# A staging transfer in two parts: four channels at the head of ScalarE's queue, four at its tail

## The chip, the cores and the metric

The kernel runs on one core of a Trainium2 chip. The time is the device time of one launch in microseconds (us). The core has engines that copy data in its on-chip memory (DVE, called VectorE, and ACT, called ScalarE), a third one (POOL, GpSimd) that here only issues transfers, and SP, which only issues transfers too. Transfers between the chip's main memory (DRAM) and the on-chip memory are carried by 16 DMA engines that all issuers share. Each issuer has a queue of its own; in the profile q10 is ScalarE's, q1 is SP's and q0 is POOL's.

## The reference

`x` holds 16 images of 64 channels of 64 x 64 float32 values. The result holds, for each of 15 x 15 window positions, the 8 x 8 window of all 64 channels; neighbouring windows overlap by half.

```python
n_h = (h - window_size) // stride + 1      # 15
n_w = (w - window_size) // stride + 1      # 15
for i in range(n_h):
    for j in range(n_w):
        result[:, i, j] = x[:, :, i*4 : i*4 + 8, j*4 : j*4 + 8]
```

There is no arithmetic. 16.8 MB are read and 59.0 MB are written (16 x 15 x 15 x 64 x 64 values of 4 bytes); the work is to cut windows out of rows and to lay them one after the other.

## The kernel before

The on-chip memory has 128 partitions. The tile `Lt` (viewed as `L`) holds all of `x`: partition = half of the channels (`ch`, 2) x group of eight images (`y`, 2) x image in the group (8) x quarter of the rows (`q`, 4), and in each partition 32 channels of 16 rows of 64 values. So one channel of one image and one quarter is a run of 4 KB in DRAM and in `L`.

Loading has two ways.

- Most channels are loaded straight into `L` by the function `load` (line 61). SP's queue takes channels 10 to 31 of the first half (`ch` 0), POOL's queue takes channels 8 and 9 of the first half and channels 7 to 31 of the second. These run over `y` and, inside, over `q`: first all four quarters of the first eight images, then those of the last eight. SP issues 14 of them and POOL 16.
- The first eight channels of the first half and the first seven of the second (`FC = (8, 7)`) are *staged*: they are loaded into the tile `GG` by eight transfers (line 129), one per quarter and half, each over all 16 images. The four transfers of `ch` 0 (8 channels, 512 KB each) are issued by ScalarE, the four of `ch` 1 (7 channels, 448 KB each) by SP. They stand at the head of both queues. Staged channels are then *moved* from `GG` into `L` by 16 copies of at most two channels (`moves`, line 148): first the four of `y` 0, `ch` 0, then `y` 0, `ch` 1, then the same for `y` 1. Every third of these copies, beginning with the first, is done by ACT, the others by DVE. A copy takes all four quarters of its two channels, so it waits for all four transfers of its half.

Windows are then gathered from `L` into output tiles, which lie in the same `GG` (the first three have 4096 values per partition, the later ones 6144, three at a time in rotation), and stored. The function `first` (line 200) fills the first three tiles with eight copies each, `plain` (line 245) and `cross` (lines 157, 258, 262) the following ones, `second` (line 228) two late ones; all of these are stored by POOL with an indirect transfer (`scatter`, line 165). The last two tiles (line 290) are stored by SP (line 291). `first` reads rows of the first eight images (`y` 0) of both halves, so it waits for the direct loads of `y` 0 and for their moves; and since its tiles lie where staged channels lay, it also waits for the moves that read those.

The order on each engine is that of the program text for the copies marked `keep_in_program_order`. A transfer's completion is counted in a semaphore. SP and ScalarE together have eight such semaphores, given out in the order of the program: the ninth transfer takes the first one's, and is issued only when that earlier transfer has landed. POOL has eight of its own.

The lines that matter below are 124 (the views `S` of the staged channels), 126 to 129 (the staging transfers), 61 (direct loads), 148 (moves), 200 and 165 (first tiles and their stores). `TC`, the name that the change uses, is 4: the number of channels whose run of 1024 values makes up one tile of 4096.

Of the kernel before, what the change touches and what calls it, by code (L numbers as in the profile page):

```python
# [10 lines left out]
def kernel(  # L11
# [7 lines left out]
    nc = tc.nc  # L19
    P = nc.NUM_PARTITIONS  # L20

    B, C, H, W = x.shape
# [8 lines left out]
    CH = 2  # L31
    HQ = P // (B * CH)
# [8 lines left out]
    QP = YB * HQ  # L41
# [75 lines left out]
    TC = CFREE // (RB * W)  # L117


    FC = (8, 7)  # L120
# [2 lines left out]
    assert sum(FC) * CP <= NG * LF  # L123
    S = [GG[:, ch * FC[0] * CP : (ch * FC[0] + FC[ch]) * CP].rearrange("p (c f) -> p c f", c=FC[ch])[:, :, 0 : RB * W].rearrange("p c (r w) -> p c r w", r=RB) for ch in range(CH)]
    x_b = x.rearrange("b (ch cl) (hq r) w -> ch hq b cl (r w)", ch=CH, hq=HQ)
    for q in range(HQ):
        for ch in range(CH):
            s = S[ch][QP + q : QP + q + (B - 1) * HQ + 1 : HQ]
            (nc.scalar, nc.sync)[ch].dma_start(out=s, in_=x_b[ch, q, :, 0 : FC[ch], :])

# [194 lines left out]
```

## Time and profile before

| | |
|---|---|
| time, median of 3 runs | 184.44 us (184.37 to 184.56) |
| the profiled execution's own time | 184.26 us |
| its span (first to last instruction) | 182.4 us |
| busy: DVE, ACT, POOL | 137.2, 138.5, 39.7 us |
| DMA: moved in the span, mean rate | 75.80 MB, 416 GB/s |

The profiled execution spends 1.86 us outside its span. The kernel's time in other runs lies up to 0.3 us above that execution's. "DMA share" in a table of stretches is the mean busy share of the 16 DMA engines; it can read a little above 1, since packets that follow one another overlap in the records by a few nanoseconds. A row of the timeline gives start, length, engine, line, operation, output and input, count, and in brackets the idle time before it and what ended it.

### The profile page before, as it was taken

To read this page: it belongs to the slowest core of one execution; us is meant where nothing else is said; L and a number is where in the kernel's file an instruction comes from. 1 tells how busy PE (TensorE), PEld (TensorE's weight loads), DVE (VectorE), ACT (ScalarE), POOL (GpSimd) and SP (SyncE) were. 2 spreads that over 40 slices of the span, in tenths; PEclk is the share of its full clock that TensorE was granted. 3 is DMA by queue.
4 is the path that set the end of the run, shared out by engine and by line. 5 is a ranking of instruction groups with operands and counts; after the bars stand their busy time and mean duration, and the time that the engine had idled before them with its cause. 6 is when DMAs were issued, how large, how long until landed. Compare 5 with 4: busy or idle time off the path is not lost.

```text
span 182.4 us, 445 instructions
## 1 busy us (share of the span) xinstructions
DVE 137.2 (75%) x138; ACT 138.5 (76%) x60; POOL 39.7 (22%) x41
## 2 busy tenths in 40 slices
DVE  4003997999995969769979979889597996996600
ACT  0003998999949978769969969889699999998600
POOL 7501553033220220220220221022207025140000
DMA  5999999999999999999999999999999999999995
GB/s 157 406 412 411 410 412 410 410 412 445 420 438 449 431 437 431 431 431 428 431 431 431 431 431 422 431 437 431 431 426 431 431 431 437 426 431 431 431 431 226
DMA packets 9363, 75.80 MB, mean 416 GB/s; under 512 B 2736, under 2 KB 2736, under 8 KB 6832
## 3 DMA queue, kind: packets, MB, share of 16 engines
q0 software_dynamic: 6592, 62.92, 81.4%
q1 hardware_dynamic: 2192, 10.75, 14.3%
q10 hardware_dynamic: 576, 2.10, 3.1%
q14 instruction: 3, 0.02, 0.0%
HBM read 16.78 MB, written 62.91 MB: 437 GB/s over the span
## 4 chain that ended last, share of the span: by engine, by line
DMA 72%; DVE 14%; issue 5%; POOL 2%; DVEq 1%; POOLq 0%; PEldq 0%
DMA out_dram<-GG,idx 23%; DMA out_dram<-GG,idx_lo 22%; DMA Lt<-in_x_dram 20%; DVE GG L157 7%; DMA out_dram<-GG,idx_hi 6%; DVE GG L200 2%; DVE GG L262 2%; POOL Lt L61 2%; DVE GG L290 2%; DVE GG L245 1%; DVEq L322 1%; DVE GG L228 0%; DVEq L245 0%; POOL pi L77 0%; DVEq L157 0%
## 5 line engine op out<-in xcount | busy, mean ns | idle before, releaser
L258 ACT COPY GG<-Lt 64x4096 f32<-64x4096 f32 (+1 forms) x20 | 55.0, 2750 | 9.7 <-DMA out_dram<-GG,idx_lo 6.2
L157 DVE STREAM_SHUFFLE GG<-Lt 64x2048 f32<-64x2048 f32 (+1 forms) x25 | 49.2, 1970 | 0.6
L245 ACT COPY GG<-Lt 64x4096 f32<-64x4096 f32 (+1 forms) x10 | 27.5, 2750 | 4.5 <-DMA out_dram<-GG,idx_v 2.7
L148 DVE COPY Lt<-GG 32x2048 f32<-32x2048 f32 (+1 forms) x10 | 11.3, 1180 | 13.8 <-DMA GG<-in_x_dram 13.7
L262 DVE COPY GG<-Lt 64x2048 f32<-64x2048 f32 (+1 forms) x20 | 19.1, 955 | 0.5
L200 DVE COPY GG<-Lt 32x2048 f32<-32x2048 f32 x15 | 18.3, 1219 | 1.3 <-DMA Lt<-in_x_dram 1.0
L228 ACT COPY GG<-Lt 32x4096 f32<-32x4096 f32 (+1 forms) x6 | 18.2, 3033 | 0.3 <-DMA out_dram<-GG,idx_hi 0.2
L228 DVE COPY GG<-Lt 32x2048 f32<-32x2048 f32 (+1 forms) x10 | 16.5, 1646 | 2.4 <-DMA out_dram<-GG,idx 1.4
L200 ACT COPY GG<-Lt 32x2048 f32<-32x2048 f32 x9 | 17.1, 1897 | 1.0 <-DMA Lt<-in_x_dram 0.8
L61 POOL DMA_DIRECT2D Lt<-in_x_dram x16 | 12.7, 798 | 17.1 <-DMA Lt<-in_x_dram 16.6
L165 POOL DMA_INDIRECT out_dram<-GG,idx x5 | 9.7, 1931 | 24.7 <-ACT GG L245 20.8
L148 ACT ACT_TABLE_LOAD x1 | 1.3, 1283 | 16.8 <-DMA GG<-in_x_dram 16.8
L245 DVE COPY GG<-Lt 64x4096 f32<-64x4096 f32 x5 | 11.4, 2289 | 0.2
L165 POOL DMA_INDIRECT out_dram<-GG,idx_hi x5 | 4.8, 961 | 30.5 <-DVE GG L262 30.5
L290 DVE COPY GG<-Lt 32x2560 f32<-32x2560 f32 (+1 forms) x8 | 9.2, 1152 | 1.8 <-DMA out_dram<-GG,idx 1.7
L148 ACT COPY Lt<-GG 32x2048 f32<-32x2048 f32 (+1 forms) x6 | 10.3, 1752 | 0.1
L165 POOL DMA_INDIRECT out_dram<-GG,idx_lo x5 | 4.8, 961 | 25.2 <-DVE GG L262 15.8
L290 ACT COPY GG<-Lt 32x1536 f32<-32x1536 f32 (+1 forms) x8 | 9.2, 1149 | 0.8 <-DMA out_dram<-GG,idx 0.6
L157 DVE LOAD_MASK_SELECT GG<-Lt x25 | 0.2, 9 | 12.6 <-DMA out_dram<-GG,idx_lo 7.3
L165 POOL DMA_INDIRECT out_dram<-GG,idx_v x3 | 4.5, 1512 | 14.3 <-DVE GG L200 8.7
L165 POOL DMA_INDIRECT out_dram<-GG,idx_r x2 | 2.8, 1403 | 11.7 <-ACT GG L228 11.7
L80 DVE TENSOR_SCALAR tb<-pi 128x1 int32<-128x1 int32 x1 | 0.2, 154 | 1.0 <-POOL pi L77 1.0
(24 smaller groups left out, 3.4 us busy)
## 6 DMA issues: line engine op xcount, KB each, us to landing
Lt<-in_x_dram POOLq DMA_DIRECT2D x8, 800.0 KB, 16.4
out_dram<-GG SPq DMA_DIRECT2D x2, 1536.0 KB
Lt<-in_x_dram SPq DMA_DIRECT2D x6, 384.0 KB
GG<-in_x_dram ACTq DMA_DIRECT2D x4, 512.0 KB
Lt<-in_x_dram SPq DMA_DIRECT2D x6, 320.0 KB
GG<-in_x_dram SPq DMA_DIRECT2D x4, 448.0 KB
Lt<-in_x_dram SPq DMA_DIRECT2D x2, 704.0 KB
Lt<-in_x_dram POOLq DMA_DIRECT2D x8, 64.0 KB, 16.4
```

The source lines that it names most:

```text
L61: eng.dma_start(out=L[p0 : p0 + QP - HQ + 1 : HQ, c0:c1, :, :], in_=x_v[ch, y, q, :, c0:c1, :])
L80: nc.vector.tensor_scalar(out=d[:, :], in0=pi[:, :], scalar1=shift, scalar2=mask, op0=ALU.logical_shift_right, op1=ALU.bitwise_and)
L148: tc.keep_in_program_order(copy(out=L[d, c:e, :, :], in_=S[ch][f, c:e]))
L157: return nc.vector.stream_shuffle(out=out, in_=in_, mask=mask)
L165: st = nc.gpsimd.indirect_dma_start(out=rows, out_offset=bass.IndirectOffsetOnAxis(ap=ix[:, 0:1], axis=0), in_=g, in_offset=None, element_ ...
L200: (act if n % 3 == 0 else dve)(out=g[d * QP : (d + 1) * QP, ch], in_=L[f : f + QP, :, s * ST : s * ST + WS, cols],)
L228: (act if i in (0, 5, 6) else dve)(out=g[d * QP : (d + 1) * QP, n], in_=windows(slice(f, f + QP), every, slice(s * ST, s * ST + WS), j, m),)
L245: tc.keep_in_program_order(copy(out=g[d, n], in_=windows(f, every, slice(half * ST, half * ST + WS), j, m)))
L258: act(out=g[lo, n], in_=windows(f, every, slice(s * ST, s * ST + WS), j, m))
L262: dve(out=g[hi, n, :, 0:ST], in_=windows(f, every, slice((s + 1) * ST, RB), j, m))
L290: copy(out=g[d, n, c0:c1], in_=windows(f, slice(c0, c1), slice(s * ST, s * ST + WS), j, m))
L322: with _tile.TileContext(nc) as tc:
```

## The change

ScalarE's first staging transfer (quarter 0 of `ch` 0) carries channels 0 to 3 in place of 0 to 7. Channels 4 to 7 of that quarter are carried by a fifth transfer, which ScalarE issues after its other three. SP's four staging transfers, all direct loads, the moves and everything behind them have the same text as before.

```diff
     x_b = x.rearrange("b (ch cl) (hq r) w -> ch hq b cl (r w)", ch=CH, hq=HQ)
-    for q in range(HQ):
-        for ch in range(CH):
-            s = S[ch][QP + q : QP + q + (B - 1) * HQ + 1 : HQ]
-            (nc.scalar, nc.sync)[ch].dma_start(out=s, in_=x_b[ch, q, :, 0 : FC[ch], :])
+    for q, ch, c0, c1 in [(q, ch, 0, TC if q + ch == 0 else FC[ch]) for q in range(HQ) for ch in range(CH)] + [(0, 0, TC, FC[0])]:
+        s = S[ch][QP + q : QP + q + (B - 1) * HQ + 1 : HQ, c0:c1]
+        (nc.scalar, nc.sync)[ch].dma_start(out=s, in_=x_b[ch, q, :, c0:c1, :])
```

In the built program two things follow from the count of nine transfers in place of eight ahead of the direct loads. The fifth transfer is the ninth on the eight shared semaphores, so it waits until ScalarE's first has landed; and each of SP's direct loads waits for a transfer that stands one place later in the program than before. And a copy of channels 0 to 3 now waits only for the first four transfers of ScalarE's queue, a copy of channels 4 to 7 for the last four.

## The prediction

> **What bounds the kernel now.** I read the page first, then the table of stretches, then the transfers by queue in the first microseconds, then the instructions around the staged copies. From the page, the DMA row (the span in 40 slices, busy tenths) and the rate:
>
> ```profile
> span 182.4 us, 445 instructions
> DVE 137.2 (75%) x138; ACT 138.5 (76%) x60; POOL 39.7 (22%) x41
> DMA  5999999999999999999999999999999999999995
> DMA packets 9363, 75.80 MB, mean 416 GB/s; under 512 B 2736, under 2 KB 2736, under 8 KB 6832
> DMA 72%; DVE 14%; issue 5%; POOL 2%; DVEq 1%; POOLq 0%; PEldq 0%
> ```
>
> DVE and ACT are idle a quarter of the span; the DMA engines are busy in every slice but the first and the last, and carry 72% of the chain that ended last. The table of stretches (columns: stretch, length, busy time of DVE, ACT, POOL, clock, DMA share, GB/s) says how full they are:
>
> ```profile
> 2.00:5.00 3.00, 1.08 (x11) 0.00 (x0) 3.00 (x6) 1.00 0.91 298
> 5.00:15.00 10.00, 0.00 (x0) 0.00 (x0) 2.15 (x4) 1.00 1.03 411
> 15.00:29.00 14.00, 11.35 (x10) 11.61 (x7) 5.67 (x6) 1.00 1.03 410
> 29.00:43.00 14.00, 13.44 (x12) 13.54 (x8) 3.65 (x3) 1.00 1.03 411
> 43.00:58.00 15.00, 14.26 (x10) 12.24 (x5) 3.24 (x3) 1.00 1.02 434
> 58.00:180.00 122.00, 96.16 (x87) 101.10 (x42) 21.11 (x16) 1.00 1.01 432
> ```
>
> From 5 to 180 us the share is 1.01 or more: there is no idle DMA time that an earlier copy could fill. The time is the bytes by their rate, plus what is lost at the two ends. Loads run at 411 GB/s to about 43 us, stores at 432 after that. So an edit to the loads can act in three ways only: it makes the beginning better or worse, it delays a store so far that the engines run dry, or it adds bytes. The change adds no byte.
>
> The beginning, 2 to 5 us, moves 298 GB/s where 411 is the rate later: 3.0 x (1 - 298/411) = 0.82 us are lost there in all, part of it before the first packet. That is the most that a better beginning can give. By queue (q10 ScalarE's, q1 SP's; first the answer for 2.0 to 3.8 us, then for 3.8 to 5.0):
>
> ```profile
> DMA packets 99, 0.41 MB, mean 225 GB/s; under 512 B 0, under 2 KB 0, under 8 KB 99
> q10 hardware_dynamic: 99, 0.41, 83.8%
> ```
>
> ```profile
> DMA packets 136, 0.49 MB, mean 406 GB/s; under 512 B 17, under 2 KB 17, under 8 KB 136
> q1 hardware_dynamic: 91, 0.37, 76.8%
> q10 hardware_dynamic: 45, 0.12, 24.8%
> ```
>
> Up to 3.8 us only ScalarE's first transfer moves, though SP issued its own at the same time; then SP's follows. The first transfer is the one that the change halves, so this is the place to look at.
>
> **The change part by part.** The rows of the staging transfers and of who waited for them, and those of the copies that use them:
>
> ```profile
> L129 ACTq DMA_DIRECT2D GG<-in_x_dram x4: 613/639/680, 0.7 to 2.7; - x4
> L129 SPq DMA_DIRECT2D GG<-in_x_dram x4: 694/764/812, 0.7 to 3.1; - x4
>   ACT L148: 16.8, 1
>   DVE Lt L148: 13.7, 1
> ```
>
> ```profile
> 16.83 1.28 ACT L148 ACT_TABLE_LOAD   x1 [16.83 <-DMA GG<-in_x_dram]
> 16.86 11.42 DVE L148 COPY Lt<-GG 32x2048 f32<-32x2048 f32 x10 [13.68 <-DMA GG<-in_x_dram]
> 18.13 10.40 ACT L148 COPY Lt<-GG 32x2048 f32<-32x2048 f32 x6
> 29.30 17.26 ACT L200 COPY GG<-Lt 32x2048 f32<-32x2048 f32 x9 [0.78 <-DMA Lt<-in_x_dram]
> 29.33 16.09 DVE L200 COPY GG<-Lt 32x2048 f32<-32x2048 f32 x13 [1.04 <-DMA Lt<-in_x_dram]
> ```
>
> *A fifth issue on ScalarE's queue.* One more issue of 0.64 us (median of the four). It waits until ScalarE's first transfer has landed; SP's first direct load waits for that landing now and goes out at 4.83 us, so it landed by then:
>
> ```profile
> 4.83 0.81 SPq L61 DMA_DIRECT2D Lt<-in_x_dram  x1
> 6.26 0.68 SPq L61 DMA_DIRECT2D Lt<-in_x_dram  x1
> 10.42 0.68 SPq L61 DMA_DIRECT2D Lt<-in_x_dram  x1
> ```
>
> Half as many bytes land no later, so the fifth is out by 4.83 + 0.64 = 5.5 us at the latest. Behind it on ACT stands only the table load, which waits until 16.8 us. Cost nothing; the cover is 11 us of idle ACT, and 1.31 MB that ScalarE's queue still has to move by then (2.10 less the 0.41 + 0.12 moved by 5 us and the fifth's own 0.26).
>
> *SP's direct loads wait one place later.* The first now goes when SP's own first transfer has landed, 6.26 us at the latest by the second row, in place of 4.83; the second takes the place of the third, and so on. SP's queue holds 4 x 448 KB = 1.84 MB of staging ahead of them, and by the next answer it moves 1.81 MB from 5 to 15 us, so it still has work to about 13 us. Cost nothing; by then three loads are in it (10.42 us). POOL's order and waits are unchanged.
>
> *When the staged channels arrive.* From 5 to 15 us, and from 15 to 17, the queues move (packets, MB, share):
>
> ```profile
> q1 hardware_dynamic: 506, 1.81, 45.3%
> q10 hardware_dynamic: 418, 1.55, 38.1%
> q0 software_dynamic: 475, 0.74, 19.7%
> ```
>
> ```profile
> q10 hardware_dynamic: 14, 0.02, 3.2%
> ```
>
> ScalarE's queue runs at 0.155 MB per us, and 0.26 MB of it moves from the front to the back: 1.7 us of that queue. If its end stays where it is, the first four transfers are in at 16.83 - 1.7 = 15.1 us and the fifth at 16.8; if the queue is set back by the whole of it, they are in at 16.8 and 18.5. I take the middle, 16.0 and 17.6, since SP's queue moves ahead at the start and gives the time back later. Then ACT loads its table at 16.0 and makes its first copy at 17.3, its second needs the fifth transfer (there), so it ends at 28.5 - 0.8 = 27.7. DVE makes one copy (1.2 us) at 16.0, waits to 17.6, and goes on where it now stands at 16.86 + 1.2 = 18.1: it ends at 28.3 - 0.5 = 27.8. In the late case DVE ends at 28.3 + 0.4 = 28.7, ACT where it does now.
>
> *What is late next.* Both then wait for direct loads to 29.3 us in every one of these cases, 0.5 to 1.7 us longer than now, or DVE 0.4 shorter in the late case. The loads' bytes ahead of that point are the same, on engines that are full, so 29.3 stays. The gain of 0.5 to 0.8 us is worth nothing. Even a slip there would not show at once: POOL issues the first stores at
>
> ```profile
> 36.37 1.76 POOL L165 DMA_INDIRECT out_dram<-GG,idx_v  x1 [5.60 <-DMA Lt<-in_x_dram]
> 42.50 1.81 POOL L165 DMA_INDIRECT out_dram<-GG,idx_v  x1 [4.38 <-DVE GG L200]
> 48.67 0.97 POOL L165 DMA_INDIRECT out_dram<-GG,idx_v  x1 [4.35 <-DVE GG L200]
> ```
>
> and from 38.2 to 43.4 us all 793 packets are under 8 KB, that is loads of 4 KB (the rows of a store have 16):
>
> ```profile
> DMA packets 793, 2.14 MB, mean 411 GB/s; under 512 B 272, under 2 KB 272, under 8 KB 793
> ```
>
> So the first store, issued by 38.1, starts behind the loads at about 43.4. Each holds 2.1 MB, 4.8 us at 434 GB/s: the second is needed at 48.2 and issued by 44.3, the third at 53.0 and issued by 49.6. The tightest cushion is 3.4 us; POOL's first load was issued at 1.5 us and has no packet in the answer for 2 to 5 us, so up to about 2.8 us of it can be the way from issue to packet, which leaves 0.6 us at worst.
>
> *The beginning.* ScalarE's first transfer now covers the engines for half as long: 0.26 MB at 411 GB/s is 0.64 us less. This is the one term that the trace does not show, so I bound it. From above: SP's queue might be unable to start before 3.8 us, and nothing else is there; the engines then stand from the end of the four channels to 3.8. ScalarE's queue alone had 0.41 MB done by then, so 0.26 MB at about 3.1 to 3.3, and the loss is up to 0.6 us. From below: the low rate might come of one queue working alone, and end when the second joins 0.64 us sooner. In finer stretches,
>
> ```profile
> 2.00:2.60 0.60, 0.57 (x8) 0.00 (x0) 0.60 (x2) 1.00 0.75 116
> 2.60:3.20 0.60, 0.52 (x4) 0.00 (x0) 0.60 (x2) 1.00 0.89 259
> 3.20:3.80 0.60, 0.00 (x0) 0.00 (x0) 0.60 (x2) 1.00 0.88 300
> 3.80:4.40 0.60, 0.00 (x0) 0.00 (x0) 0.60 (x2) 1.00 1.02 403
> ```
>
> the stretch 3.2 to 3.8 would run at 403 in place of 300, a gain of 0.6 x 103/411 = 0.15 us; with all that is lost after 2.6 us it is 0.6 x (152 + 111)/411 = 0.4 us. I take -0.1 us: the engines are already 0.88 busy with the one queue, and nothing shows SP's queue as not ready, since it was issued at 0.74 us like ScalarE's.
>
> Here the Trainium skill has a rule (DMA: Bandwidth & Descriptors, section Queues, rings and completion order): a DMA engine goes round the queues, but drains a whole packet, typically 9 to 17 descriptors, from one before it turns to the next. The trace agrees in that ScalarE's 512 KB, eight rows of 4 KB for each of 16 engines, go almost whole before SP's begin at 3.8 us. By the rule SP's transfer waits for its turn, not for readiness, and the first term above is 0 rather than 0.6 us; the forecast stands without it.
>
> **Sum.** Issue 0, waits 0, copies 0, beginning -0.1 (from -0.4 to +0.6): 184.26 - 0.1 for an execution like the profiled one, and against the median of the runs, 184.44, which is 0.18 above it, 184.35 us. Its own range: 184.0 to 184.7.
>
> **The rivals.** A measurement of this kernel can tell about 0.2%, 0.37 us, from no change.
>
> 1. *The engines stand at the beginning* (slower). SP's first transfer is not ready when the four channels are through, and ScalarE's second is not either. For it: no packet of SP's before 3.8 us in the trace. Against it: SP's transfer was issued 3 us before that. Price up to 0.6, likely 0.5 us: 184.9. It decides from a gap of 0.37 us.
> 2. *The moves become late* (slower). The fifth transfer shares its last stretch with POOL's queue and lands later than 18.5 us. It decides when the first gather starts more than 0.6 us after 29.3, so when DVE's moves end after 29.9, the fifth landing at about 19.7 or later; then a store is late by the excess. With a landing at 20.5 it is 0.8 us: 185.2. Against it: full engines, and no byte more ahead of it.
> 3. *The beginning gets better than I take it* (faster): one queue alone is what holds the rate at 116 to 300 GB/s. 0.4 us less: 184.0. For it: 403 GB/s as soon as SP's queue joins. Against: the rate climbs while ScalarE's queue is still alone, so time has a part in it.
> 4. *The smaller transfer costs its fixed time on the engines* (slower). SP's first direct load goes 4.83 - 0.74 = 4.1 us after the transfer whose landing it awaits was issued, and 0.52 MB at 411 GB/s are 1.3 of them; if a transfer's remaining 2.8 us occupied engines, one more transfer would give 187.2. Against it: share 1.03 at 411 GB/s from 5 to 15 us, with transfers of three queues in flight, so this time is covered. The Trainium skill (same page, section Anatomy of one DMA) puts it at about 2.0 us per transfer, an estimate of 186.4 by its figure; and its section Rules for kernel authors asks for at least 1 MiB per transfer, which speaks against halving one.
>
> **How the numbers follow.** Forecast 0.65, rival 1 0.12, rival 2 0.04, rival 3 0.17, rival 4 0.02. Slower by over 0.2% is 0.12 + 0.04 + 0.02 = 0.18, faster 0.17, within 0.65. The range takes the forecast's 184.0 to 184.7 and reaches to rivals 3 and 1 with a margin for their sizes: 183.85 to 185.05.
>
> **What would show it.** Right: ACT's table load at 15.1 to 16.8 us, a gap in DVE's moves behind the first, their end at 27.8 (to 28.7), the first gather at 29.3 after a longer wait for loads, first store at 36.4, DMA share 1.01 or more from 5 to 180 us. Rival 1: SP's first packets still at 3.8 us and a DMA share well under 0.88 from 3.2 to 3.8. Rival 3: over 330 GB/s in 2 to 5 us, and every later mark earlier by the same amount. Rival 2: the first gather after 29.9 and a stretch under 430 GB/s between 43 and 58 us. Rival 4: under 405 GB/s from 5 to 15. Wrong altogether I would be if the steady rates, 411 and 432 GB/s, moved: nothing in the change touches them.

## The result and the profile after

The changed kernel takes 185.11 us (median; 184.72 to 185.36), the kernel before 184.49 (184.32 to 184.59) on the same chip: a ratio of 1.0031, 95% interval 1.0020 to 1.0042. It is slower by about 0.6 us, just outside the predicted range. Its profiled execution took 184.79 us, 1.86 us of them outside its span. The page, and the table of stretches with the columns of before:

```profile
span 182.9 us, 445 instructions
DVE 137.4 (75%) x138; ACT 138.5 (76%) x60; POOL 37.0 (20%) x41
DMA  4999999999999999999999999999999999999994
```

```profile
2.00:5.00 3.00, 1.08 (x11) 0.00 (x0) 3.00 (x6) 1.00 0.90 311
5.00:15.00 10.00, 0.00 (x0) 0.00 (x0) 2.15 (x4) 1.00 1.03 409
15.00:29.00 14.00, 11.38 (x10) 11.61 (x7) 5.83 (x6) 1.00 1.04 410
29.00:43.00 14.00, 13.14 (x11) 13.33 (x8) 2.52 (x3) 1.00 1.03 411
43.00:58.00 15.00, 14.65 (x11) 12.41 (x5) 3.63 (x3) 1.00 1.03 435
58.00:180.00 122.00, 96.22 (x87) 101.16 (x42) 19.00 (x16) 1.00 1.00 431
```

Nothing here is slower by more than 2 GB/s: the beginning is a little better (311 GB/s, 298 before), and the DMA engines are full from 5 to 180 us at nearly the same rates. In the trace the last completion of a transfer (the *landing* of the last store) is recorded at 181.57 us, where it was 181.48: 0.09 later. Yet the span ends 0.53 us later (182.93 against 182.40). The difference lies behind the last byte. SP's instructions of the closing part (line 322, the program's end) from 181 us on, before and after:

```profile
L322 SPq EVENT_SEMAPHORE  x3: 17/17/28, 181.5 to 182.3; - x3
L322 SPq DRAIN  x3: 7/7/7, 181.6 to 181.9; - x3
```

```profile
L322 SPq EVENT_SEMAPHORE  x10: 17/28/28, 181.6 to 182.9; - x10
L322 SPq DRAIN  x3: 7/7/13, 182.1 to 182.4; - x3
```

Seven more semaphore instructions stand there (their durations are in ns: least, median, most). SP ends the program by waiting for every semaphore in use, two at a time, in a fixed order. What it waited for, before and after (us in total, times, longest):

```profile
SPq L322 <- DMA out_dram<-GG,idx_r: 5.3, 1, 5.3
SPq L322 <- DMA out_dram<-GG: 3.4, 1, 3.4
```

```profile
SPq L322 <- DMA out_dram<-GG: 9.1, 1, 9.1
```

Before, SP works down the list while the last stores are still moving: it stops 5.3 us for POOL's last store, and the last store of all stands at the end of the list, in the ninth pair, where it costs 3.4 us. After, the second pair already holds the last store's semaphore. SP stands there for 9.1 us, and the other seven pairs, all fulfilled by 178.1 us, are worked off behind the last landing. In the trace they begin about 0.062 us apart (181.589, 181.651, 181.715 and so on): 7 x 0.062 = 0.43 us. With the 0.09 of the landing that is the whole 0.53.

Why the place changed: SP and ScalarE hand out eight semaphores in turn. With 24 transfers the last store has the eighth; a 25th transfer, wherever it stands, gives it the first. The two traces show this by the semaphores' numbers: the last store counts on 116 before, which stands in SP's ninth and last pair, and on 100 after, the one that ScalarE's first transfer had, which stands in the second pair.

The landmarks of the copies, to compare with the lines of before:

```profile
15.62 1.28 ACT L148 ACT_TABLE_LOAD   x1 [15.62 <-DMA GG<-in_x_dram]
15.65 11.46 DVE L148 COPY Lt<-GG 32x2048 f32<-32x2048 f32 x10 [12.47 <-DMA GG<-in_x_dram]
16.92 10.40 ACT L148 COPY Lt<-GG 32x2048 f32<-32x2048 f32 x6
29.52 17.25 ACT L200 COPY GG<-Lt 32x2048 f32<-32x2048 f32 x9 [2.19 <-DMA Lt<-in_x_dram]
29.63 18.66 DVE L200 COPY GG<-Lt 32x2048 f32<-32x2048 f32 x15 [2.53 <-DMA Lt<-in_x_dram]
```

The moves are 1.2 us earlier, and the first gather is 0.2 to 0.3 us later.

### The profile page after: what moved, and what is told of

It is laid out like the page before. It is cut to its first block, busy times and chain, and to the rows that moved or that the text cites. A ratio compares the mean times of both kernels' runs of the same rounds, so it can differ in the third digit from the quotient of the medians.

```text
span 182.9 us, 445 instructions
## 1 busy us (share of the span) xinstructions
DVE 137.4 (75%) x138; ACT 138.5 (76%) x60; POOL 37.0 (20%) x41
## 4 chain that ended last, share of the span: by engine, by line
DMA 60%; DVE 16%; issue 7%; ACT 7%; ACTq 1%; DVEq 1%; SPq 1%; POOLq 0%
DMA out_dram<-GG,idx 22%; DMA out_dram<-GG,idx_lo 22%; DMA GG<-in_x_dram 7%; DVE GG L157 7%; DMA out_dram<-GG,idx_hi 7%; DVE GG L200 5%; ACT Lt L148 4%; ACT GG L200 3%; DVE GG L262 2%; DMA Lt<-in_x_dram 2%; DVE GG L290 2%; DVE GG L245 1%; ACTq L129 1%; DVEq L322 1%; SPq L61 1%
## 5 line engine op out<-in xcount | busy, mean ns | idle before, releaser
L61 POOL DMA_DIRECT2D Lt<-in_x_dram x16 | 12.2, 770 | 16.8 <-DMA Lt<-in_x_dram 16.3
L165 POOL DMA_INDIRECT out_dram<-GG,idx x5 | 7.5, 1501 | 24.3 <-ACT GG L245 20.5
```

What stands on the lines that cost most here:

```text
L61: eng.dma_start(out=L[p0 : p0 + QP - HQ + 1 : HQ, c0:c1, :, :], in_=x_v[ch, y, q, :, c0:c1, :])
L165: st = nc.gpsimd.indirect_dma_start(out=rows, out_offset=bass.IndirectOffsetOnAxis(ap=ix[:, 0:1], axis=0), in_=g, in_offset=None, element_ ...
```

## The experiments

The theory to test: the loss is the closing list, 0.062 us for each pair that stands behind the last store's. Its rivals: the new order of staging costs (a gap at the beginning, late moves), or a further transfer costs by itself.

**Another look at the changed kernel.** No edit.

> The changed kernel once more. Its nine times lay in two groups, 184.7 to 184.8 and 185.1 to 185.4, and the profiled execution was one of the first. Theory of the closing waits (SP ends the program by waiting for all semaphores in a fixed order; with one transfer more the last store counts on the semaphore that stands early in that order, so the rest of the list, about 0.06 us a pair, comes after the landing): +0.43 us over the kernel before in every run, so the second group needs a cause of its own. If this profile falls into the second group, its span is 183.2 to 183.5 and the extra 0.4 us must show as a stretch in which the DMA share falls below 1, or as a longer tail. Theory of a bad beginning: 2 to 5 us at under 298 GB/s.

184.83 us (184.77 to 185.32), ratio 1.0021 (1.0010 to 1.0032) to 184.52 before. The profiled execution was one of the slower ones, 185.26 us. Ten semaphore instructions again stand behind the landing, but the landing itself is at 182.04:

```profile
L322 SPq EVENT_SEMAPHORE  x10: 17/28/28, 182.1 to 183.3; - x10
```

Of the last packets of the last store, by which each of the 16 DMA engines ends, fifteen end by 181.14 us and one at 181.69. The span is 0.47 us longer than in the first profile of this kernel, the landing is 0.47 us later, and the closing part is the same. So in this execution the later time is one late DMA engine, not another length of the closing part; that every time of the second group has this cause is not shown. A spread of this size does not come with the change: the kernel before ran from 184.22 to 184.93 us in the 31 runs of this comparison. Take 0.43 off the nineteen times of the changed kernel and they lie at 184.29 to 184.93, the same band.

**The count restored, the new staging kept.** One direct load fewer is cut in two.

```diff
 (changed kernel)
-    SMALL, SPLIT = 2, 6
+    SMALL, SPLIT = 2, 5
```

> The changed kernel with one direct load fewer cut in two (SPLIT 5 in place of 6), so that SP and ScalarE issue 24 transfers as before the change, and the last store counts on the last semaphore again. Closing waits: 0.4 us faster than the changed kernel, 184.5 to 184.7, and the last closing wait ends within 0.1 us of the last landing. Theory that the staging order itself costs (a gap at the beginning, late moves): no faster than the changed kernel, 185.1.

184.56 us, ratio 1.0003 (0.9993 to 1.0014, that is -0.13 to 0.26 us): level with the kernel before. The list ends as before,

```profile
L322 SPq EVENT_SEMAPHORE  x3: 17/17/28, 181.6 to 182.4; - x3
```

The rival that the staging order costs falls: the order is that of the change, and the loss is gone.

**The count raised, the old staging kept.**

```diff
 (kernel before)
-    SMALL, SPLIT = 2, 6
+    SMALL, SPLIT = 2, 7
```

> The kernel before, staging untouched, with one direct load more cut in two (SPLIT 7), so 25 transfers. Closing waits: 0.4 us slower than before, 184.9 (185.1 if the second group of times belongs to the count too), with eight pairs of waits after the last landing. Theory that the staging order costs: 184.5, no change.

185.04 us, ratio 1.0029 (1.0020 to 1.0039), the loss of the change without the change:

```profile
L322 SPq EVENT_SEMAPHORE  x10: 17/28/28, 181.8 to 183.1; - x10
```

Its landing, at 181.83 us, is a late one again: one DMA engine's last packet ends at 181.49 us, those of the others by 181.19.

**The second half directly behind the first.** The first staging transfer is cut as in the change, but nothing is moved to the end.

```diff
-    ... [(q, ch, 0, TC if q + ch == 0 else FC[ch]) for q in range(HQ) for ch in range(CH)] + [(0, 0, TC, FC[0])]:
+    ... [(0, 0, 0, TC), (0, 0, TC, FC[0])] + [(q, ch, 0, FC[ch]) for q in range(HQ) for ch in range(CH)][1:]:
```

> The first staging transfer cut in two as in the change, but the second half issued directly behind the first, not at the end; 25 transfers. Closing waits: as the changed kernel, 184.9 to 185.1. Theory that moving four channels to the end of ScalarE's queue costs: 184.5. Theory of a beginning with too little cover: 184.5, since the same eight channels are at the head of the queue.

184.75 us, ratio 1.0014 (1.0004 to 1.0024, that is 0.07 to 0.44 us): slower than before, by less than expected. The closing part is the same (ten instructions, 0.43 us); the landing, 181.51, is an early one. With one direct load fewer cut, so 24 transfers:

```diff
-    SMALL, SPLIT = 2, 6
+    SMALL, SPLIT = 2, 5
```

> Both halves of the first staging transfer at the head of the queue and one direct load fewer cut (SPLIT 5), 24 transfers. Closing waits: 0.4 us faster than the same with 25, about 184.35, so level with the kernel before; the profile would show whether the shorter first transfers gain anything at the beginning (then 0.1 us below before). Theory that the cut first transfer costs: 184.75 as with 25.

184.63 us, ratio 1.0006 (0.9997 to 1.0015), three closing instructions. The interval is -0.06 to 0.28 us, so no gain from the shorter first transfers can be told at the end.

**Fewer transfers.** 21, so that the last store has the fifth semaphore.

```diff
 (kernel before)
-    SMALL, SPLIT = 2, 6
+    SMALL, SPLIT = 2, 3
```

> The kernel before, staging untouched, with three direct loads fewer cut in two (SPLIT 3), so 21 transfers of SP and ScalarE; the last store counts on the fifth of the eight semaphores. Closing waits: three pairs of waits stand behind the last landing in place of none, 3 x 0.062 = 0.19 us slower than before, about 184.7; in the profile the closing waits end 0.25 to 0.3 us after the last landing (0.08 with 24 transfers, 0.52 with 25). Theory that the number of transfers itself costs (each has a fixed price on the engines): with three fewer, faster than before by about three times what one cost, 183 to 184.1.

185.04 us, ratio 1.0027 (1.0017 to 1.0036). The rival that each transfer has a price by itself falls for these few: three fewer are slower. The closing part is as expected, three pairs:

```profile
L322 SPq EVENT_SEMAPHORE  x6: 17/28/28, 181.8 to 182.8; - x6
```

The time is 0.3 us above what was expected of it, and the trace has that in a landing at 181.79 us, again one engine (181.43, the others by 181.02). All ten times lie above 184.85 us, where the twenty of the kernel before reach 184.70. So this 0.3 us is no chance of one execution; one trace alone ties it to a late engine, and why fewer cuts give it was not found.

**The kernel before, another look at its tail.**

> The kernel before once more, for its tail: its times spread from 184.2 to 184.9 with nothing changed. If one late DMA engine makes this spread, as in the slower look at the changed kernel (15 engines done by 181.14, one at 181.69), the last landing moves with the time while the closing waits behind it stay at 0.08 us.

184.37 us, landing at 181.59, three closing instructions: an execution like the first. An execution of this kernel from the upper end of its band was not caught in a trace, so what makes its spread is not shown.

**More transfers.** All eight staging transfers cut (32 in all, the last store on the eighth semaphore again), and four of them cut (28, on the fourth).

```diff
-    ... [(q, ch, 0, TC if q + ch == 0 else FC[ch]) for q in range(HQ) for ch in range(CH)] + [(0, 0, TC, FC[0])]:
+    ... [(q, ch, c0, min(c0 + TC, FC[ch])) for q in range(HQ) for ch in range(CH) for c0 in (0, TC)]:
```

> All eight staging transfers cut in two, each half directly behind the other, direct loads as before the change: 32 transfers of SP and ScalarE, four full turns of the eight semaphores, so the last store counts on the last one as in the kernel before. Closing waits: no pair after the landing, they end 0.08 us behind it; 184.5, no slower than before in spite of eight transfers more. Theory that a further transfer costs about 0.5 us: 188.

For 28 the same line reads:

```diff
+    ... [(q, ch, c0, c1) for q in range(HQ) for ch in range(CH) for c0, c1 in ([(0, TC), (TC, FC[ch])] if q < 2 else [(0, FC[ch])])]:
```

> Four of the eight staging transfers (quarters 0 and 1 of both halves) cut in two, direct loads as before the change: 28 transfers, the last store on the fourth of the eight semaphores. Closing waits: four pairs behind the landing, 4 x 0.062 = 0.25 us, they end 0.33 us after it; 184.75. With 21 transfers the time came out 0.3 us above this rule because the landing itself was late (181.79); here direct loads are untouched, so if that came from them the landing is at 181.5 to 181.6 again. Theory that a further transfer costs: 186.

190.31 us, ratio 1.033 (1.028 to 1.038), and 188.48, ratio 1.021 (1.019 to 1.023): both far off the expectation of the times. The closing part did what it should, here for 32 and then for 28:

```profile
L322 SPq EVENT_SEMAPHORE  x3: 17/17/28, 186.6 to 187.4; - x3
```

```profile
L322 SPq EVENT_SEMAPHORE  x7: 17/28/28, 185.4 to 186.5; - x7
```

What came on top begins with the loads. With 32 transfers, from the table of stretches, the DMA row of 5 to 15 us (40 slices) and the timeline:

```profile
5.00:15.00 10.00, 0.00 (x0) 0.00 (x0) 2.14 (x4) 1.00 1.01 363
DMA  9966778898999999999999999999999999999999
DMA packets 1928, 3.63 MB, mean 363 GB/s; under 512 B 1042, under 2 KB 1042, under 8 KB 1928
2.72 8.69 ACTq L129 DMA_DIRECT2D GG<-in_x_dram  x5
13.80 15.57 SPq L61 DMA_DIRECT2D Lt<-in_x_dram  x14
58.46 2.81 POOL L165 DMA_INDIRECT out_dram<-GG,idx  x1 [5.84 <-ACT GG L245]
60.00:62.00 2.00, 0.89 (x3) 1.98 (x2) 1.27 (x1) 1.00 0.48 205
58.00:100.00 42.00, 33.12 (x36) 35.71 (x14) 8.60 (x7) 1.00 0.96 409
100.00:140.00 40.00, 34.22 (x33) 34.30 (x14) 5.78 (x6) 1.00 1.00 422
```

The last two stretches in the second profile of the kernel before:

```profile
58.00:100.00 42.00, 33.93 (x38) 35.62 (x15) 5.76 (x6) 1.00 1.00 432
100.00:140.00 40.00, 33.88 (x31) 34.81 (x13) 7.69 (x7) 1.00 1.01 433
```

The loads run at 363 GB/s in place of 411, SP's first direct load goes at 13.80 us in place of 4.83, the fourth store at 58.46 in place of 53.46 us, and then the DMA engines do run dry, at 60 to 62 us. By the rates, about 1.6 us are lost up to 29 us (363 and 397 GB/s in place of 411 and 410) and 3.3 us from 58 to 140 us, behind the late stores. Why the loads are slow was not isolated. Each of the eight semaphores serves one transfer in flight, so eight small transfers hold few bytes; for this speaks the busy share of 0.6 to 0.8 from 5.5 to 7 us. But over the ten microseconds the share is 1.01, and 1042 of the packets are under 512 B, where the kernel before had 397: the engines were also busy while they moved less. These two do not test the price of a transfer as such, but they show that eight or four transfers more are not free.

**The dose.** The end of the span less the start of the wait that the last landing released, from the traces:

| pairs behind the last store's | kernels | us |
|---|---|---|
| 0 | before, twice; 24 with the new order, with the second half adjacent; 32 | 0.90, 0.90; 0.91, 0.90; 0.90 |
| 3 | 21 | 1.09 |
| 4 | 28 | 1.15 |
| 7 | changed, twice; 25; 25 with the second half adjacent | 1.34, 1.34; 1.34; 1.34 |

A straight line with about 0.062 us per pair, whatever the load order was. This is the part that is shown. The medians differed by 0.62 us in the first comparison and by 0.31 in the second; beside the 0.43 that leaves 0.19 and -0.12. The intervals of the two ratios, 0.37 to 0.77 and 0.18 to 0.59 us, both hold 0.43.

## Why the prediction was wrong

- **The step that failed** is "an edit to the loads can act in three ways only: it makes the beginning better or worse, it delays a store so far that the engines run dry, or it adds bytes". There is a fourth: it changes what the program still does when the last byte has landed. The sum ended with the last transfer at about 180 us and took the two microseconds behind it as fixed. They are not: 0.43 us of them hang on which semaphore the last store counts on. For the median the sum with that term is 184.35 + 0.43 = 184.78, where 185.11 was measured and 184.83 in the second comparison. From the one profiled execution to the other it is 184.26 + 0.43 + 0.09 for the later landing = 184.78, where 184.79 was measured; the gain of 0.1 does not appear in it.
- **"SP's direct loads wait one place later"**, at a "Cost nothing", was right for the loads, and was the place to see it: the same shift goes on to the last two transfers of the program, and was not followed there.
- **The fifth issue** cost nothing, as said. It was out by 4.7 us, ahead of the 5.5 that the prediction gave:

```profile
4.14 0.56 ACTq L129 DMA_DIRECT2D GG<-in_x_dram  x1
```

- **The arrival of the staged channels** came at the early end of what was given: the table load at 15.62 us (15.1 to 16.8), and DVE made its ten copies without a wait for the fifth transfer, done at 27.1 us. The queue's end nearly stayed where it was (its last packet ends at 16.15 us, 15.94 before); the middle value allowed for a larger setback.
- **"What is late next"** held, with a slip. The loads landed no later, yet the first gather began at 29.52 and 29.63 us, 0.2 and 0.3 later than before. The cause is the same in small: ACT and DVE wait for a list of semaphores, and the load that lands last now counts on one that stands early in it. In the trace the last count on it is at 29.07 us (29.20 before), and five pairs of waits follow, about 0.08 us apart on ACT and 0.10 on DVE, where none followed before. With 25 transfers by one more cut load, where the staging has its old count, the gather is at 29.30 again; with 24 transfers and the new staging it is at 29.56. As forecast, the slip cost nothing: the first store was issued 0.4 us later (36.77 us), and its packets begin at 43.54 us (43.59 before). The margin for this was read too wide. That POOL's queue shows no packet from 2 to 5 us makes the way from issue to packet at least 2.8 us, not up to 2.8; in the trace its first packet begins at 5.67 us, 3.4 us after its issue ended, which is all of the tightest cushion.
- **The beginning** was sized rightly where it lies: 311 in place of 298 GB/s over 3 us is 3.0 x 13/411 = 0.09 us gained, against -0.1. The further traces agree, with 306 and 309 GB/s for the new staging order and 281 to 295 for the old. At the end of the program the gain could not be told: with the count restored the time is level, within -0.13 to 0.26 us. In the finer stretches (and, last, SP's queue from 2.0 to 3.2 us),

```profile
2.60:3.20 0.60, 0.51 (x4) 0.00 (x0) 0.60 (x2) 1.00 0.78 253
3.20:3.80 0.60, 0.00 (x0) 0.00 (x0) 0.60 (x2) 1.00 1.02 410
q1 hardware_dynamic: 3, 0.01, 4.5%
```

  the rate reaches 410 one stretch earlier, and SP's queue moves 0.01 MB by 3.2 us, where it had none by 3.8. Over all eleven traces its first packet begins at 2.95 to 3.21 us where ScalarE's first transfer has four channels, with the other four directly behind it or not, and at 3.87 to 3.95 us where it has eight; SP issued at 0.74 us in all of them. So it had been ready, and waited for its turn behind ScalarE's first transfer. That is the rule of the Trainium skill (DMA: Bandwidth & Descriptors, section Queues, rings and completion order), by which an engine drains a packet of one queue before it turns to the next; the trace agrees.
- **Rival 1** (a gap at the beginning) is excluded by these rows, and that the time lies near its 184.9 is a coincidence. **Rival 2** did not happen: the moves were earlier. **Rival 3**'s gain was there in the size of the forecast, not 0.4 us. **Rival 4** is excluded for one transfer: 409 GB/s from 5 to 15 us, where 411 stood before, and neither its 187.2 nor its 186.4 us came. One transfer more with the old staging cost 0.52 us, 0.43 of them behind the landing.

## What to carry to other kernels

When the transfers fill the span, the end of the program is part of the sum: read what each engine does behind the last landing. Where a program waits for all its semaphores in a fixed order, the last store belongs on the one that is waited for last, and any transfer that is added or removed before it, on queues that share the semaphores, moves it. The count can be restored at another place, as one direct load cut fewer did here, and then such an edit can be judged by what it was made for. The right place alone is not enough: with 32 transfers the last store had it, and the time was 190.31 us.

## What the runs showed of the hardware

A wait on two semaphores that have long been reached still takes about 0.062 us of SP; on ACT about 0.08 and on DVE about 0.10. Where the semaphore that is still open stands second in such a pair, the wait lies inside the row of the profile (5.3 us for POOL's last store); where it stands first, the wait lies ahead of a row of 0.028 us (3.4 and 9.1 us for the last store). One of the 16 DMA engines can end 0.3 to 0.55 us behind the other fifteen (0.55 in the second profile of the changed kernel, 0.4 with 21 transfers, 0.3 with 25), and between the two profiles of the changed kernel this moved the span by 0.47 us; what decides it stays open. A queue whose transfer was issued at 0.74 us had its first packet only at 3.0 us behind a first transfer of 256 KB on another queue, and at 3.9 us behind one of 512 KB. Cutting all staging transfers in two, which adds no byte, took the time from 184.46 to 190.31 us.
